# Attention on two 64-row halves of the TensorE array: scores and maximum's pass with one head of a pair on each half

## The chip, the cores and the metric

One NeuronCore of one Trainium2 chip runs the whole program. The metric is the device time of one execution in microseconds; the median of three runs is compared.

## The reference

Two layers of a diffusion backbone over 1024 latent tokens with a prefix of 256 context tokens, model width 1024, all in float32. Layer 0 mixes by recurrent heads and Fourier groups. Layer 1 is latent attention, and it alone is touched by the change. Cut to what matters:

```python
qc, kvc, kr, g = split(u @ w_in)              # 256, 128, 32, 1024 columns
q = rms_norm(qc) @ w_uq                       # 16 heads: 64 plain + 32 rotary dims
kv = rms_norm(kvc) @ w_ukv                    # 16 heads: 64 key dims + 64 value dims
q = concat(q[:64], rope(q[64:]))              # latent tokens only
k = concat(kv[:64], rope(kr))                 # rotary key: one for all heads
s = einsum('bqhd,bkhd->bhqk', q, k_all) * 96 ** -0.5   # 1024 queries x 1280 keys
o = softmax(s) @ v_all
y = (o * silu(g)) @ w_out
```

The layer ends with a gated residual and a layer norm; the output is the latent stream (1, 1024, 1024).

## The kernel before, in words

Everything is written with tile pools; a scheduler orders each engine's instructions and places the semaphores, starting from the order of the program text. Products that need float32 accuracy run as three float32r passes: both operands are split into a high and a low part (`split`, L85: a copy by one engine, L81 or L83, and a subtraction by another, L87), and high x high, high x low and low x high are summed (`mm3`, L89 to 92).

The stage of the gate columns (L977 to 994, line groups in1g) multiplies 8 blocks of weights by the latent activations, 384 matmuls of 512 columns in all. Between its steps a list `work` of closures prepares the first pair of heads (L973 to 975): weights and rotated queries of a quad of four heads (`prep_quad`), keys and queries of a pair (`prep_pair`), the maximum's pass (`max_pass`) and the quad's values (`prep_v`).

The attention (L1078 to 1126) runs over 8 pairs of heads, two halves of 512 queries, and 10 key tiles of 128 keys: 160 steps of `attend`. Keys lie on partitions of the scores. For each head of the pair a PSUM bank `s` takes three matmuls: high keys by high queries over 97 rows (64 plain dims, 32 rotary dims, and a row of ones in the keys that meets the negated maximum in the queries), high keys by low queries and low keys by high queries over 96 rows (L1021 to 1023). ScalarE's exponential writes a tile `p` (L1025; six buffers for each head), GpSimd adds it to the row sum `ra` (L1029), and P*V runs in plain float32 on two column halves of the array, one head on each (`tile_position=(0, 64 * a)`, L1034), in groups after the key tiles that `PVG` names (1, 3, 5, 7, 8) and after the last one. `finish` multiplies the row sums by ones on column halves (`rp`, L1059), inverts them on VectorE in four pieces (`ri`, L1066), multiplies by the gate (`sgt`, L1061 and L1070) and stores.

While a pair attends, the closures of the next pair are spread over the first 18 of its 20 steps, by the weights that stand beside them in the lists (L1087 to 1091). For odd `p` a new quad is prepared too. Each half of a pair thus has its own load: the first half holds the quad's rotations and the pair's keys and queries, the second mostly the maximum's pass and, with a quad, the values.

The pieces of a pair's preparation: `kn`, three chunks of keys (512, 512, 256 columns), each an `mm3` into one bank of `m_ps`, then for each head a 64-row split by ScalarE and VectorE; `qn`, two chunks of queries in the same way; `qr`, VectorE copies of the rotary queries (32 rows of 1024) into the rows 64 to 95 of `Qh` and `Ql` (L933, L934). The maximum's pass takes, for each head and each tile of 128 queries, the high x high scores against 512, 512 and 256 keys, one bank each (L955), reduces each bank to a maximum (L956) and the three to one (L957). `rows` transposes the maxima, negates them and sends them by a GpSimd DMA to the row 96 of `Qh` (L967).

PSUM has eight banks: four in `m_ps` (all preparations and the maximum's pass share them), three in `s_ps`, one in `o_ps`. The operands of a pair lie in `slots`: those of even pairs in the pool `prep`, those of odd pairs in the pool `at`. The pool `prep` is closed before the last pair (L1093). In the last pair nothing is prepared; instead `wo1_load` (L1101 to 1109) loads the output weights in eight pieces, multiplies them by the gate and splits them, all on VectorE, into tiles of a pool that is opened where `prep` lay, with two buffers `raw` for the pieces on their way. Loads and stores run on SyncE's queue (SP, `load`, L65).

Of the kernel before, what the change touches and what calls it, by code (L numbers as in the profile page):

```python
# [21 lines left out]
P = 128  # L22
# [32 lines left out]
MB = 4  # L55
SB = 3
# [3 lines left out]
def _body(ctx, tc, ap, out, dbg=None):  # L60
# [36 lines left out]
    # ---------------------------------------------------------------- constants  # L97
# [13 lines left out]
    # v = 8 softplus(-lambda): softplus(x) = max(x, 0) + log1p(exp(-|x|)),  # L111
    # log1p(e) = 2 atanh(e / (2 + e))
# [26 lines left out]
    # the channel DFT folded into the group weights  # L139
# [9 lines left out]
    # ---------------------------------------------------------------- adaLN  # L149
    # stationary: the silu of the two condition vectors, 32 columns (two used)  # L150
# [60 lines left out]
    # layer 0 by quarters of the channels, so that the projection can start on the first  # L211
# [4 lines left out]
    def ada_part(h):  # L216
# [12 lines left out]
        # chunk 2 s + i of shift (s = 0) and scale (s = 1): channel block 2 h + i  # L229
# [82 lines left out]
    # ---------------------------------------------------------------- RG-LRU heads  # L312
# [78 lines left out]
    # x projections run one head pair ahead of the gates that use them  # L391
# [3 lines left out]
    nop = lambda: None  # noqa: E731  # L395
# [435 lines left out]
    def slots(p, i0):  # L831
        for i in (i0, i0 + 1):
# [472 lines left out]
```

## Time and profile before

| | |
|---|---|
| median of 3 runs | 1498.38 us (1496.85 to 1505.64) |
| the profiled execution, first to last instruction | 1498.8 us |
| TensorE busy | 1434.9 us (96%) |
| VectorE, ScalarE, GpSimd busy | 1037.0, 571.7, 706.4 us |
| gate stage | 722 to 831 us |
| attention | 831 to 1400 us |

Busy times are unions of what the profiler recorded for an engine. A matmul's recorded end is modelled and lies behind the start of the next one, so the time that a matmul takes from a row of matmuls is read from start to start. PEld are weight loads. "Idle before" is the time that an engine stood before an instruction, with the instruction that ended the wait.

### The profile page before, as it was taken

Reading aid. Unit: us, or ns where it says so; the run is one execution under the profiler, and the core shown is the slowest. Engines: PE = TensorE matmul, PEld = TensorE weight load, DVE = VectorE, ACT = ScalarE, POOL = GpSimd, SP = SyncE. Lnnn points to the kernel's source line nnn. Section 1 sums busy time; section 2 is a strip of 40 time slices with the busy share of each in tenths; the row PEclk is TensorE's granted clock in tenths of the full one; section 3 lists DMA queues with packets and bytes.
Section 4 is the critical chain, followed back from the end, with each engine's and each line's share of the span. In section 5 each row is a group of like instructions: output and inputs, shape, how many; then the busy total and the mean of one; then the engine's idle time right before and its main releaser. Section 6 shows DMA issues by size and latency. Waiting matters only on the chain.

```text
span 1498.8 us, 18430 instructions
## 1 busy us (share of the span) xinstructions
PE 1434.9 (96%) x6880; PEld 1040.1 (69%) x6880; DVE 1037.0 (69%) x1636; ACT 571.7 (38%) x840; POOL 706.4 (47%) x460
## 2 busy tenths in 40 slices
PE   6998999999999999999999999999999999998898
PEld 3776777778888788879888655655566556554586
DVE  4669778765765243348675769787977787779498
ACT  2276565665113221124321544443444334443110
POOL 1135434343212154213411676677667756689652
PEclk9999999999999999999999999999999989999999
DMA  8613233332304653310231101010100000022542
GB/s 302 229 52 107 99 105 109 109 102 85 111 29 147 211 168 115 119 37 26 95 106 50 60 15 43 15 32 22 36 15 15 29 14 15 15 71 71 181 135 91
DMA packets 63641, 127.05 MB, mean 85 GB/s; under 512 B 5304, under 2 KB 31160, under 8 KB 61248
## 3 DMA queue, kind: packets, MB, share of 16 engines
q1 hardware_dynamic: 60592, 117.82, 24.1%
q0 software_dynamic: 2528, 7.67, 1.4%
q8 instruction: 54, 0.88, 0.3%
q10 hardware_dynamic: 432, 0.39, 0.1%
q14 instruction: 35, 0.29, 0.1%
HBM read 101.14 MB, written 24.66 MB: 84 GB/s over the span
## 4 chain that ended last, share of the span: by engine, by line
PE 72%; DVE 20%; DMA 3%; issue 2%; ACT 2%; POOL 1%; SPq 0%; DVEq 0%; ACTq 0%; POOLq 0%
PE z L272 13%; PE y L651 10%; PE po L1034 8%; PE yf L1167 6%; PE mx L955 5%; PE s L1021 4%; PE s L1023 4%; PE s L1022 4%; PE in1g L92 2%; PE in1g L90 2%; PE in1g L91 2%; DVE xc L322 2%; DVE th L367 1%; DVE gate L372 1%; DVE ri L1066 1%
## 5 line engine op out<-in xcount | busy, mean ns | idle before, releaser
L1029 POOL TENSOR_TENSOR ra<-ra,p 128x512 f32<-128x512 f32 x256 | 351.4, 1399 | 96.2 <-ACT p L1025 95.8
L1025 ACT ACTIVATE p<-s 128x512 f32<-128x512 f32 x320 | 190.1, 597 | 249.9 <-PE s L1023 222.2
L956 DVE TENSOR_REDUCE m<-mx 128x1 f32<-128x512 f32 (+1 forms) x384 | 207.8, 591 | 55.1 <-PE mx L955 53.8
L272 PE MATMUL z<-uh,w0h 128*128 128x512 f32 (+1 forms) x576 | 150.0, 367 | 4.3 <-ACT uh L81 4.3
L87 POOL TENSOR_TENSOR w0l<-w,w0h 128x1024 fp32r<-128x1024 f32 x24 | 63.9, 2664 | 184.5 <-DVE w0h L83 126.4
L272 PE MATMUL z<-uh,w0l 128*128 128x512 f32 (+1 forms) x576 | 147.7, 362 | 0.0
L272 PE MATMUL z<-ul,w0h 128*128 128x512 f32 (+1 forms) x576 | 147.7, 362 | 0.0
L1021 PE MATMUL s<-Qh,Kh 97*128 97x512 f32 x320 | 132.5, 414 | 6.3 <-ACT p L1025 6.3
L1022 PE MATMUL s<-Ql,Kh 96*128 96x512 f32 x320 | 128.1, 400 | 0.0
L1023 PE MATMUL s<-Qh,Kl 96*128 96x512 f32 x320 | 128.1, 400 | 0.0
L955 PE MATMUL mx<-Kh,Qh 96*128 96x512 f32 (+1 forms) x384 | 115.8, 376 | 7.9 <-DVE Ql L87 4.3
L272 PEld LDWEIGHTS z<-uh,w0h 128*128 128x128 f32 x576 | 98.4, 190 | 33.4 <-issue 10.7
L955 PEld LDWEIGHTS mx<-Kh,Qh 96*128 96x128 f32 x384 | 69.4, 190 | 66.2 <-issue 22.6
L272 PEld LDWEIGHTS z<-ul,w0h 128*128 128x128 f32 x576 | 96.7, 190 | 18.7 <-issue 1.0
L272 PEld LDWEIGHTS z<-uh,w0l 128*128 128x128 f32 x576 | 96.5, 190 | 18.4 <-issue 2.0
L350 ACT ACTIVATE gate<-gps,vec 128x512 f32<-128x512 f32 (+1 forms) x96 | 57.5, 616 | 103.6 <-PE gps L92 103.4
L1021 PEld LDWEIGHTS s<-Qh,Kh 97*128 97x128 f32 x320 | 60.9, 190 | 48.3 <-issue 24.9
L1034 PE MATMUL po<-p,v_even 128*64 128x512 f32 x320 | 85.9, 620 | 0.0
L1034 PE MATMUL po<-p,v_odd 128*64 128x512 f32 x320 | 82.7, 615 | 0.0
L1029 POOL TENSOR_TENSOR ra<-p,p 128x512 f32<-128x512 f32 x32 | 48.4, 1533 | 70.6 <-ACT p L1025 70.6
L386 POOL TENSOR_TENSOR gate<-gate,gate 128x1280 f32<-128x1280 f32 x8 | 23.9, 2992 | 112.2 <-DVE gate L383 97.1
L1023 PEld LDWEIGHTS s<-Qh,Kl 96*128 96x128 f32 x320 | 61.7, 193 | 15.7 <-issue 3.2
(357 smaller groups left out, 2983.3 us busy)
## 6 DMA issues: line engine op xcount, KB each, us to landing
w<-in_w SPq DMA_DIRECT2D x24, 512.0 KB, 4.4
adaw<-in_ada SPq DMA_DIRECT2D x32, 256.0 KB, 4.9
adawm<-in_ada SPq DMA_DIRECT2D x8, 1024.0 KB, 5.7
adawg<-in_ada_g SPq DMA_DIRECT2D x8, 1024.0 KB, 4.9
y_dr<-sg SPq DMA_DIRECT2D x10, 640.0 KB, 5.5
woraw<-in_wo SPq DMA_DIRECT2D x12, 512.0 KB, 3.6
xt<-in_x_cm SPq DMA_DIRECT2D x8, 640.0 KB, 6.4
yra<-y_dr SPq DMA_DIRECT2D x10, 512.0 KB, 4.8
```

Of the source, the lines that this page charges most:

```text
L87: el.tensor_tensor(out=lo, in0=src, in1=f(hi), op=ALU.subtract)
L272: TE.matmul(z[:, a : a + n], wi[:, kt, :], ui[kt][:, a : a + n], start=(kt == 0 and ui is uh and wi is wh), stop=(kt == KT - 1 and wi is wl))
L651: TE.matmul(ps[:, 512 * hf : 512 * hf + 512], a[k], b[k][:, 512 * hf : 512 * hf + 512], start=(k == 0 and a is yh and b is woh), stop=(k = ...
L955: TE.matmul(ps[:, :n], Qh[s][0:96, P * t : P * t + P], Kh[s][0:96, a0 : a0 + n], start=True, stop=True)
L956: V.tensor_reduce(out=m3[:, i : i + 1], in_=ps[:, :n], axis=AX.X, op=ALU.max)
L1021: TE.matmul(ps, Kh[s][0:97, ks], Qh[s][0:97, c], start=True, stop=False)
L1022: TE.matmul(ps, Kh[s][0:96, ks], Ql[s][:, c], start=False, stop=False)
L1023: TE.matmul(ps, Kl[s][:, ks], Qh[s][0:96, c], start=False, stop=True)
L1025: S.activation(out=e, in_=ps, func=AF.Exp, scale=SCALE)
L1029: G.tensor_tensor(out=ra, in0=st["e"][0][a] if kt == 1 else ra, in1=e, op=ALU.add)
L1034: TE.matmul(st["o"][64 * a : 64 * a + 64, :], quad[q][6][:, k, 128 * i + 64 * a : 128 * i + 64 * a + 64], st["e"][k][a], start=(k == 0), s ...
L1167: TE.matmul(ps[i], a[:, k, :], b[k][:, pieces[i]], start=(k == 0 and a is oh and b is w1o), stop=(k == 7 and a is ol))
```

## The change

The two heads of a pair lie on two halves of the array's rows: partitions 0 to 63 hold the first head, 64 to 127 the second, in `Qh`, `Ql`, `Kh`, `Kl`, which now carry the 64 plain dims alone. The rotary dims and the maximum move into tiles of their own. `KR1` holds for each half the 32 high rows of the rotary key and its 32 low rows, `R1` the high rotary query twice, so that one matmul over 64 rows gives high x high and high x low. `KR2` holds the high rotary key and rows of ones, `R2` the low rotary query and the negated maximum, over 33 rows. A step of `attend` becomes five parts, each two matmuls (one per head) on the two row halves, into the two banks of one tile `s`; one exponential, one tile `p` and one row sum serve both heads. In the last pair the sum of the second head goes to VectorE. The maximum's pass runs plain and rotary part (`Qh` x `Kh`, `R1` x `KR1`) for both heads into two banks `x`, and one reduction serves both heads. Its unit is now one chunk of keys: 24 units a pair. Splits of keys and queries take both heads at once. Rotary queries are brought by six DMAs of 32 rows on SyncE's queue, rotary keys by three. PSUM: `m_ps` has one bank `m` for the preparations and two for `x`, one buffer of each; `s_ps` two buffers of two banks. The output weights' high parts are copied by ScalarE. Lines that change comments alone are left out.

```diff
-MB = 4
-SB = 3
...
-    m_ps, m_psc = pool("m_ps", MB, space=PSUM)
-    s_ps, s_psc = pool("s_ps", SB, space=PSUM)
+    m_ps, m_psc = pool("m_ps", 1, space=PSUM)
+    s_ps, s_psc = pool("s_ps", 2, space=PSUM)
...
+    def slots(p, i):
+        Qh[i] = p.tile([P, NL], F32R, name=f"Qh{i}")
+        Ql[i] = p.tile([P, NL], F32R, name=f"Ql{i}")
+        Kh[i] = p.tile([P, T], F32R, name=f"Kh{i}")
+        Kl[i] = p.tile([P, T], F32R, name=f"Kl{i}")
+        R1[i] = p.tile([P, NL], F32R, name=f"R1{i}")
+        R2[i] = p.tile([P, NL], F32R, name=f"R2{i}")
+    def rotary_keys():
+        for a in range(2):
+            V.memset(f(KR2)[64 * a + 32 : 64 * a + 64, :], 1.0)
+        S.copy(out=KR1[64:96, :], in_=kr_t[64:96, :])
+        V.tensor_tensor(out=KR1[96:128, :], in0=kr_t[64:96, :], in1=f(KR1)[64:96, :], op=ALU.subtract)
+        load(f(KR1)[0:64, :], f(KR1)[64:128, :])
+        for a in range(2):
+            load(f(KR2)[64 * a : 64 * a + 32, :], f(KR1)[64:96, :])
     pr_p, pr_c = pool("prep", side="left")
+    KR1 = pr_p.tile([P, T], F32R, name="KR1")
+    KR2 = pr_p.tile([P, T], F32R, name="KR2")
...
     def prep_pair(p):
-                for a in range(2):
-                    split(Qh[sl[a]][0:64, c], Ql[sl[a]][0:64, c], pq[64 * a : 64 * a + 64, :], S, V)
+                split(Qh[b][:, c], Ql[b][:, c], pq, S, V)
...
         def qr():
             for a in range(2):
                 g = slice(64 * i + 32 * a, 64 * i + 32 * a + 32)
-                V.tensor_copy(out=Qh[sl[a]][64:96, :], in_=f(roth)[g, :])
-                V.tensor_copy(out=Ql[sl[a]][64:96, :], in_=f(rotl)[g, :])
+                for r in range(2):
+                    load(f(R1[b])[64 * a + 32 * r : 64 * a + 32 * r + 32, :], f(roth)[g, :])
+                load(f(R2[b])[64 * a : 64 * a + 32, :], f(rotl)[g, :])
...
-                for a in range(2):
-                    split(Kh[sl[a]][0:64, a0 : a0 + n], Kl[sl[a]][0:64, a0 : a0 + n], pk[64 * a : 64 * a + 64, :n], S, V)
+                split(Kh[b][:, a0 : a0 + n], Kl[b][:, a0 : a0 + n], pk[:, :n], S, V)
-        return [(kn(a0, n), 1.3) for a0, n in CH3] + [(qn(0), 1.5), (qr, 2.2), (qn(1), 1.5)]
+        return [(qr, 0.0)] + [(kn(a0, n), 0.9) for a0, n in CH3] + [(qn(0), 1.5), (qn(1), 1.5)]
     def max_pass(p):
-        def unit(a, t):
+        def unit(t, i):
             def run():
+                if i == 0:
+                    m3s[t] = pr_p.tile([P, 2, 3], F32, tag="m3", bufs=3, name=f"m3{p}{t}")
+                a0, n = CH3[i]
+                ps = m_ps.tile([P, 2, 512], F32, tag="x", name=f"mx{p}{t}{i}")
+                for q, k, st in ((Qh[b], Kh[b], True), (R1[b], KR1, False)):
+                    for a in range(2):
+                        r = slice(64 * a, 64 * a + 64)
+                        TE.matmul(ps[:, a, :n], q[r, P * t : P * t + P], k[r, a0 : a0 + n], start=st, stop=not st)
+                V.tensor_reduce(out=m3s[t][:, :, i], in_=ps[:, :, :n], axis=AX.X, op=ALU.max)
+                if i == 2:
+                    V.tensor_reduce(out=nm[:, :, t], in_=m3s[t], axis=AX.X, op=ALU.max)
...
-                G.dma_start(out=Qh[s][96:97, :], in_=row[8 * a : 8 * a + 8, :])
+                G.dma_start(out=R2[b][64 * a + 32 : 64 * a + 33, :], in_=row[8 * a : 8 * a + 8, :])
-        return [(unit(a, t), 2.0) for t in range(8) for a in range(2)] + [(rows, 0.5)]
+        return [(unit(t, i), 1.0 if i == 2 else 1.6) for t in range(8) for i in range(3)] + [(rows, 0.5)]
+    slots(pr_p, 0)
-    work = (work[:1] + wait + [(lambda: trq(TOKE[-1]), 0.0), (lambda: slots(pr_p, 0), 0.0)] + wait[:W2]
+    work = (work[:1] + wait + [(lambda: trq(TOKE[-1]), 0.0), (rotary_keys, 0.0)] + wait[:W2]
...
+        sp = s_ps.tile([P, 2, 512], F32, tag="s", name=f"in1g{m}")
         for q in range(2):
-            ps = s_ps.tile([P, 512], F32, tag="s", name=f"in1g{m}{q}")
+            ps = sp[:, q, :]
...
     def attend(p, hf, kt, st):
-        for a in range(2):
-            s = 2 * (p % 2) + a
-            ps = s_ps.tile([P, 512], F32, tag="s", name=f"s{p}{hf}{kt}{a}")
-            TE.matmul(ps, Kh[s][0:97, ks], Qh[s][0:97, c], start=True, stop=False)
-            TE.matmul(ps, Kh[s][0:96, ks], Ql[s][:, c], start=False, stop=False)
-            TE.matmul(ps, Kl[s][:, ks], Qh[s][0:96, c], start=False, stop=True)
...
+        ps = s_ps.tile([P, 2, 512], F32, tag="s", name=f"s{p}{hf}{kt}")
+        parts = ((Kh[b], Qh[b], 64), (Kh[b], Ql[b], 64), (Kl[b], Qh[b], 64), (KR1, R1[b], 64), (KR2, R2[b], 33))
+        for j, (k, w, n) in enumerate(parts):
+            for a in range(2):
+                r = slice(64 * a, 64 * a + n)
+                TE.matmul(ps[:, a, :], k[r, ks], w[r, c], start=(j == 0), stop=(j == len(parts) - 1))
+        es = at.tile([P, 2, 512], F32, tag="p", bufs=PB, name=f"p{p}{hf}{kt}")
+        S.activation(out=es, in_=ps, func=AF.Exp, scale=SCALE)
+        if kt:
+            ra = st["ra"]
+            for eng, h in ((G, slice(0, 2)),) if p < 7 else ((G, slice(0, 1)), (V, slice(1, 2))):
+                eng.tensor_tensor(out=ra[:, h], in0=(st["e"][0] if kt == 1 else ra)[:, h], in1=es[:, h], op=ALU.add)
...
-                    split(w1o[k], w1p[k], r, V, V)
+                    split(w1o[k], w1p[k], r, S, V)
```

## Rows read from the trace of the kernel before

**Rows 1.** The page, part 1: busy us, share of the span, instructions.
```profile
PE 1434.9 (96%) x6880; PEld 1040.1 (69%) x6880; DVE 1037.0 (69%) x1636; ACT 571.7 (38%) x840; POOL 706.4 (47%) x460
```

**Rows 2.** Windows: gate stage, then attention by half; us, busy us (instructions), clock, DMA, GB/s.
```profile
722.10:831.10 109.00, 109.00 (x504) 90.19 (x503) 66.27 (x140) 29.38 (x52) 28.00 (x23) 1.00 0.27 86
...
896.40:938.10 41.70, 38.85 (x153) 22.96 (x153) 34.90 (x54) 17.35 (x32) 24.69 (x19) 0.96 0.12 38
...
1119.10:1153.00 33.90, 33.90 (x144) 20.12 (x145) 25.74 (x45) 17.70 (x31) 26.76 (x21) 1.00 0.05 16
1153.00:1184.70 31.70, 31.70 (x136) 18.22 (x137) 23.07 (x47) 12.53 (x21) 24.48 (x21) 1.00 0.06 18
1184.70:1229.40 44.70, 41.86 (x153) 24.17 (x154) 34.99 (x54) 17.43 (x32) 24.83 (x19) 0.89 0.07 24
...
1331.80:1357.70 25.90, 25.90 (x105) 13.44 (x106) 24.37 (x18) 12.42 (x21) 23.60 (x13) 1.00 0.36 117
1357.70:1399.80 42.10, 30.42 (x105) 14.39 (x106) 32.82 (x20) 13.27 (x23) 41.24 (x25) 0.84 0.28 81
```

**Rows 3.** Timeline of TensorE, last pair: start us, us, engine line op names count.
```profile
1378.45 1.94 PE L1034 MATMUL po<-p,v_odd 128*64 128x512 f32 x8
1380.32 0.50 PE L1021 MATMUL s<-Qh,Kh 97*128 97x512 f32 x1
1380.66 0.40 PE L1022 MATMUL s<-Ql,Kh 96*128 96x512 f32 x1
1380.89 0.40 PE L1023 MATMUL s<-Qh,Kl 96*128 96x512 f32 x1
...
1386.46 0.39 PE L1023 MATMUL s<-Qh,Kl 96*128 96x512 f32 x1
1386.78 1.08 PE L1034 MATMUL po<-p,v_odd 128*64 128x512 f32 x4
1387.79 0.50 PE L1021 MATMUL s<-Qh,Kh 97*128 97x512 f32 x1
```

**Rows 4.** Tile po: count, duration ns min/median/max, first and last start.
```profile
L1034 PEld LDWEIGHTS po<-p,v_odd x320: 132/136/232, 979.2 to 1398.4; 128*64 128x64 f32 x160
L1034 PE MATMUL po<-p,v_odd x320: 592/592/1112, 979.2 to 1399.1; 128*64 128x512 f32 x160
```

**Rows 5.** Timeline of TensorE's weight loads, 1003 to 1005 us.
```profile
1003.59 0.20 PEld L1034 LDWEIGHTS po<-p,v_odd 128*64 128x64 f32 x4 [0.36 <-issue]
```

**Rows 6.** Tile mx: reductions, and what its engine waited for (us, times).
```profile
L956 DVE TENSOR_REDUCE m<-mx x384: 404/677/693, 768.9 to 1324.3; 128x1 f32<-128x512 f32 x128, 128x1 f32<-128x256 f32 x64
...
  DVE m L956: 19.0, 33
```

**Rows 7.** Groups by line, 831.1 to 1401.6 us: busy us, mean ns, idle before.
```profile
L87 DVE TENSOR_TENSOR Kl<-pk,Kh 64x512 fp32r<-64x512 f32 (+1 forms) x42 | 24.2, 596 | 4.9 <-ACT Kh L81 4.3
...
L933 DVE CAST Qh<-roth 32x1024 fp32r<-32x1024 f32 x14 | 18.8, 1342 | 0.3
...
L934 DVE CAST Ql<-rotl 32x1024 fp32r<-32x1024 f32 x14 | 15.0, 1071 | 18.5 <-PE s L1022 18.4
```

**Rows 8.** Tile sgt: its loads and stores, issue to landing.
```profile
DMA to landing us min/median/max: 2.0/2.0/2.9
```

**Rows 9.** Timeline of GpSimd, 1327 to 1401 us.
```profile
1327.50 5.01 POOL L1029 TENSOR_TENSOR ra<-ra,p 128x512 f32<-128x512 f32 x4
...
1337.94 32.33 POOL L1029 TENSOR_TENSOR ra<-ra,p 128x512 f32<-128x512 f32 x16
```

**Rows 10.** Timeline of VectorE, start of the last pair.
```profile
1332.43 0.69 DVE L1061 TENSOR_TENSOR sgt<-sgt,osb 128x512 f32<-128x512 f32 x1 [6.26 <-ACT osb L1047]
1333.92 1.23 DVE L1107 TENSOR_TENSOR w1oraw<-w1oraw,g1bc 128x1024 f32<-128x1024 f32 x1 [0.80 <-DMA w1oraw<-in_wo]
...
1336.75 2.30 DVE L1107 TENSOR_TENSOR w1oraw<-w1oraw,g1bc 128x1024 f32<-128x1024 f32 x1
```

**Rows 11.** Timeline of TensorE, end of the last pair, with idle before.
```profile
1395.01 0.80 PE L1021 MATMUL s<-Qh,Kh 97*128 97x512 f32 x1 [6.26 <-ACT p L1025]
```

More of the change, by code (lines that the diff above doesn't have):

```diff
@@ L822, in _body @@
     e_psc()
-    m_ps, m_psc = pool("m_ps", MB, space=PSUM)
-    s_ps, s_psc = pool("s_ps", SB, space=PSUM)
-    Qh, Ql, Kh, Kl = {}, {}, {}, {}
-    def slots(p, i0):
-        for i in (i0, i0 + 1):
-            Qh[i] = p.tile([97, NL], F32R, name=f"Qh{i}")
-            Ql[i] = p.tile([96, NL], F32R, name=f"Ql{i}")
-            Kh[i] = p.tile([97, T], F32R, name=f"Kh{i}")
-            Kl[i] = p.tile([96, T], F32R, name=f"Kl{i}")
-            if i == 0:
-                for t in range(NT):
-                    G.tensor_copy(out=Kh[0][96:97, P * t : P * t + P], in_=one)
-                S.copy(out=Kh[0][64:96, :], in_=kr_t[64:96, :])
-                V.tensor_tensor(out=Kl[0][64:96, :], in0=kr_t[64:96, :], in1=f(Kh[0])[64:96, :], op=ALU.subtract)
-            else:
-                e = G if i == 1 else V
-                e.tensor_copy(out=Kh[i][64:97, :], in_=f(Kh[0])[64:97, :])
-                e.tensor_copy(out=Kl[i][64:96, :], in_=f(Kl[0])[64:96, :])
+    m_ps, m_psc = pool("m_ps", 1, space=PSUM)
+    s_ps, s_psc = pool("s_ps", 2, space=PSUM)
+    Qh, Ql, Kh, Kl, R1, R2 = {}, {}, {}, {}, {}, {}
+    def slots(p, i):
[13 more added lines that the diff above has]
+            load(f(KR2)[64 * a : 64 * a + 32, :], f(KR1)[64:96, :])
     pr_p, pr_c = pool("prep", side="left")
-    one = pr_p.tile([1, P], F32, name="one")
-    V.memset(one, 1.0)
+    KR1 = pr_p.tile([P, T], F32R, name="KR1")
+    KR2 = pr_p.tile([P, T], F32R, name="KR2")
     vt = {0: pr_p.tile([P, NT, 256], F32, name="v_even")}
@@ L917, in prep_pair @@
         wh, wl, kh, kl, roth, rotl, v = quad[q]
[L918 removed]
+        b = p % 2
         def qn(hf):
@@ L1000, in _body @@
     o_ps, o_psc = pool("o_ps", 1, space=PSUM)
-    slots(at, 2)
+    slots(at, 1)
     ones = at.tile([P, 64], F32, name="ones")
@@ L1014, in attend @@
             st["o"] = o_ps.tile([P, 512], F32, tag="o", name=f"po{p}{hf}")
-            st["ra"] = [at.tile([P, 512], F32, tag=f"ra{a}", bufs=2, name=f"ra{p}{hf}{a}") for a in range(2)]
+            st["ra"] = at.tile([P, 2, 512], F32, tag="ra", bufs=2, name=f"ra{p}{hf}")
             st["e"] = []
-        es = []
-        for a in range(2):
-            s = 2 * (p % 2) + a
-            ps = s_ps.tile([P, 512], F32, tag="s", name=f"s{p}{hf}{kt}{a}")
-            TE.matmul(ps, Kh[s][0:97, ks], Qh[s][0:97, c], start=True, stop=False)
-            TE.matmul(ps, Kh[s][0:96, ks], Ql[s][:, c], start=False, stop=False)
-            TE.matmul(ps, Kl[s][:, ks], Qh[s][0:96, c], start=False, stop=True)
-            e = at.tile([P, 512], F32, tag=f"p{a}", bufs=PB, name=f"p{p}{hf}{kt}{a}")
-            S.activation(out=e, in_=ps, func=AF.Exp, scale=SCALE)
-            es.append(e)
-            if kt:
-                ra = st["ra"][a]
-                G.tensor_tensor(out=ra, in0=st["e"][0][a] if kt == 1 else ra, in1=e, op=ALU.add)
+        b = p % 2
+        ps = s_ps.tile([P, 2, 512], F32, tag="s", name=f"s{p}{hf}{kt}")
[10 more added lines that the diff above has]
+                eng.tensor_tensor(out=ra[:, h], in0=(st["e"][0] if kt == 1 else ra)[:, h], in1=es[:, h], op=ALU.add)
         st["e"].append(es)
@@ L1034, in pv @@
                 TE.matmul(st["o"][64 * a : 64 * a + 64, :], quad[q][6][:, k, 128 * i + 64 * a : 128 * i + 64 * a + 64],
-                          st["e"][k][a], start=(k == 0), stop=(k == NT - 1), tile_position=(0, 64 * a))
+                          st["e"][k][:, a, :], start=(k == 0), stop=(k == NT - 1), tile_position=(0, 64 * a))
         if pend and kt == DK:
@@ L1058, in rows @@
             for a in range(2):
-                TE.matmul(st["rp"][64 * a : 64 * a + 64, :], ones, st["ra"][a], start=True, stop=True, tile_position=(0, 64 * a))
+                TE.matmul(st["rp"][64 * a : 64 * a + 64, :], ones, st["ra"][:, a, :], start=True, stop=True, tile_position=(0, 64 * a))
             st["ri"] = at.tile([P, 512], F32, tag="ri", name=f"ri{p}{hf}")
```

10 lines of the change are left out of this document (2 added, 8 removed).

## The prediction

> **What bounds the kernel now.** I read the page's engine shares first, then the attention's halves in a table of windows, then single instructions. TensorE is busy 96% of the span [rows 1]. The stage of the gate columns (722 to 831 us) is TensorE without a gap, 109.00 us busy of 109.00 [rows 2]. In the attention the half of a pair is the unit. Halves that prepare a pair without a new quad take 33.9 and 31.7 us, all of it TensorE, with VectorE at 25.7 and 23.1 us [rows 2]. Three halves prepare a quad as well (the first and the last of them stand in the rows): 41.7, 40.2 and 44.7 us, VectorE with 35 us of work and TensorE idle for 2.8 us in each [rows 2]. The last pair is different again: 25.9, then 42.1 us with GpSimd busy 41.24 us [rows 2].
>
> So most halves are the sum of their matmuls. A 512-column score matmul takes a slot of 0.23 us (start to start), although each is recorded at 0.40 us [rows 3]. The switches into and out of the column-tiled P*V groups cost extra: the last score starts 0.32 us before the group, not 0.23 (+0.09); four P*V matmuls take 1.01 us to the next start while four more add only 0.86 (+0.15); the first score after it takes 0.34 (+0.11). Together 0.35 us a visit [rows 3].
>
> **Do two tiles of the array run side by side?** No instruction of this kernel uses row halves, but P*V uses column halves. Eight of its records take 1.87 us to the next start, 0.23 each [rows 3]. One is recorded at 592 ns [rows 4]; less the tail of 0.16 us that scores show (0.40 against 0.23) it holds its half for 0.43 us, so two overlap fully. Weight loads do too: four of 136 ns fit into 0.20 us [rows 4, 5]. I take the same of row halves and 0.005 us more a slot: 0.236 us for one step of both heads. Bounds: 0.231 (free) and 0.462 (one after the other).
>
> **The change, part by part** (sums against this execution's span, 1498.8 us; the runs' median is 1498.38, so nothing is added).
>
> *Scores.* Six slots per key tile become five: 6 x 0.231 = 1.386, 5 x 0.236 = 1.18, so 0.206 us. In pairs 0 to 6 there are 140 key tiles: **-28.8 us**. Weight loads double (ten per 1.18 us), but two halves load at once as column halves do [rows 5].
>
> *Maximum's pass.* Before, one matmul per head and chunk; now two steps that both heads share: the same TensorE time. VectorE's 48 reductions a pair become 24 over both heads. 512 columns take 677 ns and 256 take 404 [rows 6], so 1.07 ns a column: 1024 should take 1.22 us. A pair's reductions go from 32 x 0.677 + 16 x 0.404 = 28.1 us to 16 x 1.22 + 8 x 0.677 = 24.9.
>
> *VectorE.* Per pair also five splits of 64 rows fewer (5 x 0.6 = 3.0 us) and no rotary copies (2 x 1.34 + 2 x 1.07 = 4.8 us), and the 18.4 us that VectorE stood before those copies until old scores had ended go too [rows 7]. With the reductions that is 11 us a pair. The halves that prepare a quad hold about 101 slots of 0.231, 8 of 0.117, 44 of 0.217 and 7 visits of 0.35, so 36.2 us; they lose 5.5, 4.0 and 8.5 us to VectorE, 18 in all. I give back **-15** (bounds 0 and -18).
>
> *Rotary rows by DMA.* Six copies a pair on SP's queue. A load of this stage lands 2.0 us after issue [rows 8]; the first group of the maximum's pass needs it, but three key and two query products come between. For an even pair SP waits until VectorE has split the rotated queries, and the next rope tables and gate tiles queue behind; none of these is wanted sooner than some us. I count nothing; if the cover fails it is 2 us in four pairs at most.
>
> *More visits.* Key, query, rotation, value and transpose products stay on the full array and now interrupt row-tiled work. In pairs 1 to 7 that is 7 x 6 + 3 x 7 = 63 groups. Where a group follows P*V it costs half a visit, else a whole one: I take 0.28 us, **+17.6** (bounds 0.17 and 0.35 each: 11 and 22). In the gate stage, which has no slack, 24 groups of the maximum's pass sit between full-array products: 24 x 0.35 = **+8.4** (bounds 4 and 10).
>
> *One buffer for the maximum's pass.* Before, four banks turn over; now one pair of banks, and one bank for all preparations. A 512-column group holds its banks for 0.236 to its last start, 0.393 until that ends and 1.22 for the reduction, 1.85 us; a 256 one 1.07. A pair's 24 groups chain to 38 us; the four preparations ahead of the first group, one buffer each in turn (product, ScalarE copy, VectorE subtraction, about 2.1 us), add 8. VectorE's other 13 us fit between at best. That makes 46 to 59 us beside 63 us of TensorE work in a plain pair (65.6 - 4.1 + 6 x 0.3), so it fits, but not everywhere: with four buffers 33 groups already waited for the reduction, 0.58 us each [rows 6]. There are 24 units on 18 steps, so one in three is second in its step. 56 groups at half that wait: **+16** (bounds 0 and 168 x 0.58 = 97).
>
> The Trainium skill's "TensorEngine Tiling (Array Packing)", section Performance Considerations, says that tiling speeds up TensorE but not the emptying of PSUM, which may become the limit. It speaks against this edit: by it the 24 reductions set a pair's pace, the slower rival below. The plain halves before don't show it, VectorE has room there [rows 2].
>
> *Last pair.* GpSimd's 36 sums take 1.25 us alone (four in 5.01) and 2.02 here (16 in 32.33) [rows 9]; VectorE's products of two tensors take 1.23 alone and 2.30 here [rows 10]. Each waits for the other's instruction. TensorE then stands 6.26 us for exponentials that wait for buffers [rows 11], and its granted clock falls (0.84 on average over that half, so a part of it at 1.2 GHz [rows 2]). Now GpSimd keeps 18 sums (22.5 us), VectorE gets 18 (0.69 each, as its product of this size at 1332 us [rows 10]: 12.4) beside 16 x 1.23 and four short products (22.5), and ScalarE takes the 8 casts. The shared time falls from 45 + 22.5 = 67.5 us (68.0 measured) to 57, and the casts no longer delay either; TensorE's own work is 47 us. I take the middle, 52: **-16** (bounds -11 and -21). One thing goes the other way: the rotary keys lie in the pool that is closed before this pair, and the pair still reads them. If the output weights that take their place must wait, two staging buffers are held and 19.6 us of VectorE work move behind the attention, beside the first product tile's 48 slots, 11 us: then the upper end is about -5.
>
> Sum: -28.8 - 15 + 17.6 + 8.4 + 16 - 16 = -17.8, so **1481 us**.
>
> **Rivals.**
> 1. *The reductions pace the pairs (slower).* TensorE issues in order; if two groups in three wait 0.58 us, 112 x 0.58 = 65 us instead of 16: **1530 us**. It decides from 35 us of such waits on (60 groups). For it: one buffer, other VectorE work of 0.7 to 1.7 us between the reductions. Against: VectorE falls to about 38 of 63 us in a plain pair.
> 2. *No waits.* Preparations land behind P*V groups (visits 8 us cheaper), the buffers never bind (16), and the last pair is TensorE's 47 us (5 more): **1452 us**. For it: the plain halves before lose next to nothing.
> 3. *The quad halves don't relax.* The single bank for rotations and keys (7 products of some 3 us in turn, 21 us, in a third of a half) takes the place of VectorE's load: the -15 goes, **1496 us**, no measurable change.
> 4. *The halves don't overlap as hoped.* If not at all: 1.13 us more in each of 160 key tiles (181) and 9 us per maximum's pass of eight (72): 1734 us. If only in part, say 0.30 us a step because weight loads are exposed (a first score after a visit, with its load exposed, takes 0.34): 0.064 x 800 = 51 and 20 in the maximum's passes: 1552 us. Against both: the column halves overlap fully [rows 3 to 5].
>
> The Trainium skill's "TensorE: Matmul & The Clock Gate", Part 3 (Measured speedup vs the span model), gives 3.07 for four row tiles and 2.38 for three column tiles, 0.78 of the ideal. By that rule a step would take 0.231 / 0.78 = 0.296 us (an estimate), about the partial case; this trace's sustained column halves don't bear it out.
>
> **Chances.** Forecast 0.43 (its own range 1466 to 1494; a little over half of it is below the bound for faster), rival 1: 0.19, rival 2: 0.20, rival 3: 0.10, rival 4: 0.08 (0.05 in part). A measurement of this kernel can tell about 1% (15 us) from no change. Faster by over 1%: 0.25 of the forecast and rival 2, 0.45. Within 1%: the rest of the forecast, rival 3 and the lower edge of rival 1, 0.30. Slower: 0.25. The range that leaves out 2 in 10 goes from rival 2 to rival 1: 1450 to 1532.
>
> **What would show it.** Right: score matmuls in pairs a few ns apart, a pair every 0.23 to 0.24 us; plain pairs near 64 us, the quad halves near 37; VectorE waiting more and TensorE's waits before the maximum's pass near 0.1 us a group; the gate stage some 8 us longer; the last pair near 52 us. Wrong: a step of 0.3 us or more; gaps before most groups of the maximum's pass, ended by its reduction; output weights split after the last score.

## The result and the profile after

The changed kernel takes 1662.92 us (median of four runs, 1659.55 to 1665.39) against 1497.62 of the kernel before in the same session: ratio 1.1081, 95% interval 1.1041 to 1.1122. It is slower, and 131 us above the upper end of the predicted range. The profiled executions span 1657.5 and 1498.8 us, so 158.7 us are to be found.

To find them I cut each span at the same events: the first product of the gate columns, the last copy of P\*V sums (ScalarE's osb) of pair 6 and of pair 7, and the end. Every kernel of this study is listed with these three stretches (us):

| kernel | gate stage and pairs 0 to 6 | last pair | after it | span |
|---|---|---|---|---|
| before | 609.6 | 68.0 | 99.0 | 1498.8 |
| changed | 748.0 | 48.2 | 137.9 | 1657.5 |
| e1 keys open | 750.4 | 68.8 | 104.2 | 1655.1 |
| e2 short reductions | 699.0 | 48.3 | 136.2 | 1608.5 |
| e3 three banks | 686.7 | 48.2 | 137.7 | 1597.3 |
| e4 two edits, last pair | 611.2 | 61.9 | 103.2 | 1499.9 |
| e5 shared tiles, full array | 803.9 | 81.6 | 106.3 | 1720.8 |
| e6 row halves, own tiles | 650.0 | 53.9 | 136.5 | 1563.2 |
| e7 cast held back | 609.6 | 54.2 | 114.7 | 1499.9 |
| e8 held and lagged | 603.5 | 60.0 | 97.6 | 1485.3 |
| e9 e6 with the end mended | 648.6 | 66.1 | 104.1 | 1545.3 |
| e10 e6, even chunks | 646.0 | 53.9 | 137.1 | 1559.2 |

The experiments e1, e2, e3, e5, e6 and e10 were run once. In before, e4, e7 and e8 nothing is edited up to pair 6, and that stretch still differs by 7.7 us between their executions (603.5 to 611.2), so differences of that size say nothing.

The change loses 138.4 us up to pair 6, wins 19.8 in the last pair, and loses 38.9 behind it. First the page's engine shares of the changed kernel, to be held beside [rows 1]: VectorE has 78 us less to do, and still everything is later.

```profile
PE 1506.9 (91%) x7904; PEld 1018.7 (61%) x7904; DVE 958.9 (58%) x1315; ACT 535.1 (32%) x648; POOL 630.7 (38%) x304
```

The windows of the changed kernel answer to [rows 2]: the gate stage with pairs 0 to 6, one half that prepares a quad, two plain halves, the two halves of the last pair, and the gap behind it (us; then busy us of TensorE, weight loads, VectorE, ScalarE, GpSimd; granted clock; DMA share; GB/s).

```profile
723.40:1471.40 748.00, 675.15 (x3515) 360.04 (x3517) 386.97 (x489) 205.19 (x245) 336.20 (x157) 0.97 0.13 39
928.50:980.00 51.50, 44.59 (x214) 21.21 (x214) 31.38 (x37) 13.56 (x16) 22.39 (x10) 0.93 0.16 46
1210.90:1255.80 44.90, 38.91 (x207) 19.38 (x209) 23.00 (x26) 13.38 (x17) 24.72 (x12) 0.96 0.08 22
1255.80:1293.80 38.00, 32.89 (x203) 16.42 (x203) 21.13 (x26) 10.81 (x11) 22.25 (x12) 1.00 0.04 15
1471.40:1495.60 24.20, 24.20 (x146) 11.50 (x148) 14.37 (x15) 10.81 (x12) 14.80 (x10) 1.00 0.06 22
1495.60:1519.60 24.00, 23.81 (x143) 11.29 (x143) 13.86 (x15) 10.83 (x11) 13.85 (x10) 1.00 0.17 55
1519.60:1557.90 38.30, 1.08 (x4) 0.20 (x4) 23.67 (x23) 9.99 (x10) 0.69 (x1) 0.58 0.41 139
```

The kernel before in the gate stage with pairs 0 to 6:

```profile
722.20:1331.80 609.60, 599.88 (x2571) 380.81 (x2570) 453.24 (x830) 249.21 (x432) 378.03 (x295) 0.99 0.11 36
```

Of the 138.4 us lost there, TensorE's idle time makes up 63.1 (9.7 before, 72.9 now). In the other 75.3 it is recorded as busy, so waits alone are less than half of the loss.

Plain halves that were TensorE without a gap (33.9 and 31.7 us) now take 44.9 and 38.0, with idle time of 5 to 6 us in each. The timeline of TensorE in another plain half shows where it sits (start us, us recorded, engine, line, operation, names, count; in brackets idle time and what ended it):

```profile
1448.52 0.39 PE L962 MATMUL mx<-Kh,Qh 64*128 64x256 f32 x2
1448.74 0.28 PE L962 MATMUL mx<-KR,R 64*128 64x256 f32 x2
1448.86 0.39 PE L1033 MATMUL s<-Qh,Kh 64*128 64x512 f32 x2
1449.09 0.39 PE L1033 MATMUL s<-Ql,Kh 64*128 64x512 f32 x2
1449.32 0.40 PE L1033 MATMUL s<-Qh,Kl 64*128 64x512 f32 x2
1449.56 0.39 PE L1033 MATMUL s<-R,KR 64*128 64x512 f32 x1
1451.57 0.50 PE L962 MATMUL mx<-Kh,Qh 64*128 64x512 f32 x2 [1.62 <-DVE m L963]
1451.90 0.39 PE L962 MATMUL mx<-KR,R 64*128 64x512 f32 x2
```

VectorE over the same stretch, in the same columns:

```profile
1447.68 1.75 DVE L1076 RECIPROCAL ri<-rp 128x128 f32<-128x128 f32 x2
1449.47 1.44 DVE L1080 TENSOR_TENSOR sgt<-ri,sgt 128x512 f32<-128x512 f32 x1
1450.83 0.68 DVE L963 TENSOR_REDUCE m<-mx 128x2 f32<-128x512 f32 x1
```

Read the two together. The group of 1448.52 has left the array by about 1449, but its reduction starts at 1450.83, because two reciprocals and a product stand ahead of it on VectorE. Until it ends, the one buffer is held. The next group stands in TensorE's order in the middle of a key tile's scores (seven of its ten matmuls have started by 1449.56), so the other scores wait with it. The tile mx of the changed kernel shows how often (idle time of the engines before its instructions, what ended it, us and times), beside [rows 6]:

```profile
L963 DVE TENSOR_REDUCE m<-mx x192: 629/1224/1228, 765.9 to 1464.4; 128x2 f32<-128x1024 f32 x128, 128x2 f32<-128x512 f32 x64
its engine sat idle before it (us, times) until:
  PE mx L962: 168.5, 154
  DVE m L963: 144.7, 188
```

TensorE's own part of the second row:

```profile
PE mx L962 <- DVE m L963: 44.8, 80, 3.4
```

In 154 of 192 groups VectorE stands and waits for the matmuls, 168.5 us in all. The other way round a reduction is waited for 188 times, 144.7 us: 44.8 us in 80 waits of TensorE's matmuls, the rest in its weight loads. The two take turns. Behind the last pair the timeline of ScalarE shows the output weights' casts, each waiting for VectorE's product of weights that have just been loaded:

```profile
1523.56 2.17 ACT L79 CAST w1oh<-w1oraw 128x1024 fp32r<-128x1024 f32 x2 [3.36 <-DVE w1oraw L1117]
1531.72 1.04 ACT L79 CAST w1oh<-w1oraw 128x1024 fp32r<-128x1024 f32 x1 [5.98 <-DVE w1oraw L1117]
...
1556.82 1.04 ACT L79 CAST oh<-orw 128x1024 fp32r<-128x1024 f32 x1 [4.19 <-DMA orw<-o_dr]
```

The last row is the cast of the first output tile. Its load takes one of the two buffers that the weights' pieces pass through and was issued at 1552.71 us, when the pieces were split, so it comes late with them.

The timeline of TensorE shows what that costs, 36.49 us until the first output product:

```profile
1557.91 1.22 PE L1177 MATMUL yf<-w1oh,oh 128*128 128x512 f32 x2 [36.49 <-ACT oh L79]
```

### The profile page after: what moved, and what is told of

Its sections match the earlier page's. It is cut to its first block, busy times and chain, and to the rows that moved or that the text cites. A ratio compares the mean times of both kernels' runs of the same rounds, so it can differ in the third digit from the quotient of the medians.

```text
span 1657.5 us, 19613 instructions
## 1 busy us (share of the span) xinstructions
PE 1506.9 (91%) x7904; PEld 1018.7 (61%) x7904; DVE 958.9 (58%) x1315; ACT 535.1 (32%) x648; POOL 630.7 (38%) x304
## 4 chain that ended last, share of the span: by engine, by line
PE 67%; DVE 24%; DMA 3%; ACT 2%; issue 2%; POOL 1%; SPq 0%; DVEq 0%; ACTq 0%; POOLq 0%
PE z L270 12%; PE po L1044 9%; PE y L649 9%; PE s L1033 7%; DVE m L963 7%; PE mx L962 6%; PE yf L1177 6%; DVE ri L1076 2%; PE in1g L88 2%; PE in1g L89 2%; PE in1g L90 2%; DVE xc L320 2%; DVE gate L370 1%; DVE th L365 1%; PE rp L1069 1%
## 5 line engine op out<-in xcount | busy, mean ns | idle before, releaser
L1039 POOL TENSOR_TENSOR ra<-ra,p 128x1024 f32<-128x1024 f32 (+1 forms) x128 | 291.3, 2276 | 236.4 <-ACT p L1035 234.3
L963 DVE TENSOR_REDUCE m<-mx 128x2 f32<-128x1024 f32 (+1 forms) x192 | 200.3, 1043 | 168.6 <-PE mx L962 168.5
L1035 ACT ACTIVATE p<-s 128x1024 f32<-128x1024 f32 x160 | 164.0, 1025 | 374.8 <-PE s L1033 373.5
L1033 PE MATMUL s<-R,KR 33*128 33x512 f32 (+1 forms) x640 | 134.3, 405 | 0.0
L962 PE MATMUL mx<-Kh,Qh 64*128 64x512 f32 (+1 forms) x384 | 92.9, 453 | 45.2 <-DVE m L963 44.8
L1033 PE MATMUL s<-Qh,Kh 64*128 64x512 f32 x320 | 87.9, 447 | 0.0
L1033 PEld LDWEIGHTS s<-R,KR 33*128 33x128 f32 (+1 forms) x640 | 76.9, 190 | 15.7 <-issue 2.2
L1033 PE MATMUL s<-Ql,Kh 64*128 64x512 f32 x320 | 82.8, 402 | 0.0
L1033 PE MATMUL s<-Qh,Kl 64*128 64x512 f32 x320 | 79.8, 403 | 0.0
L962 PE MATMUL mx<-KR,R 64*128 64x512 f32 (+1 forms) x384 | 77.3, 360 | 0.0
```

Source lines behind the costliest of these rows:

```text
L962: TE.matmul(ps[:, a, :n], q[r, P * t : P * t + P], k[r, a0 : a0 + n], start=st, stop=not st)
L963: V.tensor_reduce(out=m3s[t][:, :, i], in_=ps[:, :, :n], axis=AX.X, op=ALU.max)
L1033: TE.matmul(ps[:, a, :], k[r, ks], w[r, c], start=(j == 0), stop=(j == len(parts) - 1))
L1035: S.activation(out=es, in_=ps, func=AF.Exp, scale=SCALE)
L1039: eng.tensor_tensor(out=ra[:, h], in0=(st["e"][0] if kt == 1 else ra)[:, h], in1=es[:, h], op=ALU.add)
```

## The experiments

**e1: the rotary keys in a pool that stays open.**

```diff
+    kr_p, kr_c = pool("keys", side="left")
+    KR1 = kr_p.tile([P, T], F32R, name="KR1")
+    KR2 = kr_p.tile([P, T], F32R, name="KR2")
     pr_p, pr_c = pool("prep", side="left")
-    KR1 = pr_p.tile([P, T], F32R, name="KR1")
-    KR2 = pr_p.tile([P, T], F32R, name="KR2")
```

> The changed kernel with the two rotary-key tiles KR1 and KR2 in a pool of their own that stays open to the end; nothing else differs. Theory A (the output weights take the place of KR1 and KR2, which the last scores still read, so the weights' casts and splits come only after the last score): the idle time of 36.5 us before the first output product goes, the stretch from the last score to the end falls from 137 to about 100 us, and the last pair grows by 0 to 4 us because weights are now split beside it; span 1657 to 1621-1630. Rival (the weights are late because their loads stand behind others on SyncE's queue, or because ScalarE and VectorE are full in the last pair): at most 10 us less, span 1647 or more, with the casts of w1oh still after the last exponential.

Measured: 1657.21 us in one run, span 1655.1. The weights do move into the last pair and what follows it falls from 137.9 to 104.2 us, as theory A had it. But the pair grows from 48.2 to 68.8 us, not by 0 to 4, so 13.1 of the 33.7 us stay (the gate stage also began 8.3 us later in this execution, which hides most of them in the span). ScalarE's timeline in e1's last pair tells why:

```profile
1499.87 1.03 ACT L1036 ACTIVATE p<-s 128x1024 f32<-128x1024 f32 x1 [0.65 <-PE s L1034]
1505.72 1.04 ACT L79 CAST w1oh<-w1oraw 128x1024 fp32r<-128x1024 f32 x1 [4.82 <-DVE w1oraw L1118]
1506.67 1.02 ACT L1036 ACTIVATE p<-s 128x1024 f32<-128x1024 f32 x1
```

Its row in the table of waits (us in total, times, longest):

```profile
ACT w1oh L79 <- DVE w1oraw L1118: 17.3, 6, 5.2
```

A cast that waits for VectorE stands ahead of exponentials: 17.3 us in six waits. The last pair's gain was that the weights were not there.

**e2: short reductions.** Most of the maximum is left out.

```diff
-                V.tensor_reduce(out=m3s[t][:, :, i], in_=ps[:, :, :n], axis=AX.X, op=ALU.max)
+                V.tensor_reduce(out=m3s[t][:, :, i], in_=ps[:, :, :64], axis=AX.X, op=ALU.max)
...
-        S.activation(out=es, in_=ps, func=AF.Exp, scale=SCALE)
+        S.activation(out=es, in_=ps, func=AF.Exp, scale=SCALE / 4)
```

> The changed kernel, where the maximum's reduction reads only the first 64 columns of each head's chunk instead of 512 or 256, so most of the maximum is left out; the exponential's scale is a quarter, so that nothing overflows. The matmuls, their weights, the visits of the pass and its buffer stay as they are; only the time for which its one PSUM buffer is held shrinks, by about 0.8 us of a mean 1.04 in 192 groups. Theory B (the one buffer makes matmuls and reduction take turns): the pairs 0 to 6 fall from 84 (plain) and 99 (quad) us to about 70 and 84, some 90 us together, and the gate stage loses 5 to 10; span 1657 to 1550-1580. Rival C (the time is in the visits themselves: changes between full, row and column modes, and products of weights by values cut in pieces): under 20 us less, span 1637 or more.

Measured: 1610.63 us; gate stage and pairs 0 to 6 take 699.0 us, 49.0 less. That is far over rival C's 20 and well short of theory B's 77 to 107. The tile mx of e2:

```profile
L963 DVE TENSOR_REDUCE m<-mx x192: 228/292/295, 769.4 to 1417.2; 128x2 f32<-128x128 f32 x192
...
  PE mx L962: 235.4, 163
```

With reductions of 0.29 us the buffer still makes the two engines take turns (VectorE waits 163 times), as the reduction's place in VectorE's order is unchanged. So shorter reductions give back half of the 98 us that the shared tiles cost (e6 below). That is more than the time for which the buffer is held: VectorE's work in this stretch also falls, from 387.0 to 253.1 us, and all that stands behind a reduction comes sooner.

**e3: three single banks.** The pass, the preparations and the row sums share a ring of three banks, each head reduced on its own.

```diff
-    m_ps, m_psc = pool("m_ps", 1, space=PSUM)
+    m_ps, m_psc = pool("m_ps", 3, space=PSUM)
...
-                ps = m_ps.tile([P, 2, 512], F32, tag="x", name=f"mx{p}{t}{i}")
+                ps = [m_ps.tile([P, 512], F32, tag="m", name=f"mx{p}{t}{i}{a}") for a in range(2)]
...
+                for a in range(2):
+                    V.tensor_reduce(out=m3s[t][:, a, i : i + 1], in_=ps[a][:, :n], axis=AX.X, op=ALU.max)
```

> The changed kernel, where the maximum's pass writes each head's scores to a one-bank PSUM tile of its own, in a ring of three banks that the preparations and row sums share (the same banks that were one for these and two for the pass); each head has its own reduction, 384 of 0.68 or 0.40 us in place of 192 of 1.22 or 0.63. Theory B (turns through one buffer): the next group's first head finds a free bank at once and the second waits only for one reduction, so a part of the turns goes: 30 to 70 us less, span 1590-1630, unless VectorE's added instructions (192 by about 0.15, 29 us in all, over seven pairs in which it is half idle) take it back. Rival C (visits): no gain, span 1650 or more.

Measured: 1599.65 us, 686.7 up to pair 6: 61.3 less, with the same number of banks and more reductions. TensorE's waits for the pass fall from 44.8 us (80 times) to 16.9, while the ring brings a new wait (TensorE's waits in e3, us in total, times, longest):

```profile
PE pk L88 <- DVE ri L1077: 17.0, 3, 5.7
PE mx L962 <- DVE m L964: 16.9, 34, 4.4
```

**e4: the two edits of the last pair alone, in the kernel before.**

```diff
-                G.tensor_tensor(out=ra, in0=st["e"][0][a] if kt == 1 else ra, in1=e, op=ALU.add)
+                (V if p == 7 and a else G).tensor_tensor(out=ra, in0=st["e"][0][a] if kt == 1 else ra, in1=e, op=ALU.add)
...
-                    split(w1o[k], w1p[k], r, V, V)
+                    split(w1o[k], w1p[k], r, S, V)
```

> The kernel before with two edits of the change alone: in the last pair the second head's row sums go to VectorE instead of GpSimd, and the output weights' first cast goes to ScalarE instead of VectorE. Scores, layouts and PSUM stay as before. Theory D (the last pair is paced by GpSimd's additions, 36 of 1.2 us, and the change's 20 us there come from these two edits and not from the row halves): the last pair falls from 68 to 48-53 us, and the time by 15 to 20 us, to 1478-1483. Rival (the last pair gains by the five steps in place of six slots and by exponentials of two heads together): the pair stays above 60 us, the time above 1490.

Measured: 1497.57 us, ratio 0.9991 (0.9967 to 1.0016): nothing. The pair takes 61.9 us instead of 68.0, and what follows 103.2 instead of 99.0. Theory D falls. The rival's numbers hold, but its reason doesn't: in e1 the five steps and shared exponentials are there and the pair takes 68.8 us. Common to both is the weights' work.

**e5 and e6: the change in two parts.** e5 puts the kernel before on the change's PSUM tiles, e6 puts the change's row halves on the tiles of before (its row sums stay over both heads). First e5, on the kernel before:

```diff
-MB = 4
-SB = 3
+MB = 1
+SB = 2
...
+                ps = m_ps.tile([P, 2, 512], F32, tag="x", name=f"mx{p}{t}{i}")
+                    TE.matmul(ps[:, a, :n], Qh[s][0:96, P * t : P * t + P], Kh[s][0:96, a0 : a0 + n], start=True, stop=True)
...
+        sp = s_ps.tile([P, 2, 512], F32, tag="s", name=f"s{p}{hf}{kt}")
+        S.activation(out=es, in_=sp, func=AF.Exp, scale=SCALE)
```

Then e6, on the changed kernel, beside e3's edit of the pass:

```diff
+    m_ps, m_psc = pool("m_ps", 4, space=PSUM)
+    s_ps, s_psc = pool("s_ps", 3, space=PSUM)
...
+        ps = [s_ps.tile([P, 512], F32, tag="s", name=f"s{p}{hf}{kt}{a}") for a in range(2)]
+            S.activation(out=es[:, a, :], in_=ps[a], func=AF.Exp, scale=SCALE)
```

> The kernel before with the change's PSUM tiles alone: both heads of a pair in one two-bank tile (two for scores, one for the maximum's pass, one bank for preparations and row sums), exponentials, row sums and reductions over both heads at once. Operands and matmuls stay on the full array, with six slots a key tile. Theory B (the turns through the pass's one buffer are the main loss): pairs 0 to 6 take 590 to 640 us in place of 501, the time is 1590-1650. Rival C (the loss comes with the row halves: changes of mode, halves that run alone): pairs 0 to 6 stay under 530 us, the time under 1535.

> The change's row halves alone: its operands and matmuls, but each head with one-bank PSUM tiles as before (four that the maximum's pass, preparations and row sums share, three for scores), exponentials and reductions by head. Theory B: without the one buffer pairs 0 to 6 come back to 490-530 us (501 before, 634 with the change), the last pair stays near 48 and the tail near 138, the time is 1505-1555. Rival C: pairs 0 to 6 stay at 560 us or more, as with three shared banks, the time at 1590 or more.

Measured: e5 1722.62 us, e6 1565.26. Theory B's side of both; e5 is worse than it said (pairs 0 to 6 alone take 694.5 us), and e6 just above its range (531.7). Gate stage and pairs 0 to 6 make a square (us):

| | four banks in a ring, scores in three | one shared buffer and one bank, scores in two pairs |
|---|---|---|
| full array | 609.6 (before) | 803.9 (e5) |
| row halves | 650.0 (e6) | 748.0 (changed) |

Sharing the tiles costs 98 us with row halves and 194 without. The halves cost 40 us where there are banks enough and give back 56 where there aren't. VectorE has less work with them (387 us against e5's 447), which may be why; no run shows it. The window of that stretch in e5, where the granted clock is 0.92:

```profile
729.00:1532.90 803.90, 727.95 (x2565) 405.74 (x2565) 447.41 (x561) 225.54 (x285) 345.95 (x167) 0.92 0.09 28
```

TensorE's largest wait in it, summed:

```profile
PE mx L959 <- DVE m L960: 33.5, 28, 2.2
```

The same window and waits of e6:

```profile
722.80:1372.80 650.00, 616.12 (x3517) 361.58 (x3517) 391.29 (x692) 214.89 (x393) 336.88 (x157) 0.98 0.15 45
```

```profile
PE pq L88 <- DVE ri L1077: 16.0, 3, 5.3
PE mx L962 <- DVE m L964: 9.2, 17, 1.7
```

With four banks the pass waits 9.2 us in 17 places, but the queries of three quads still wait 5.3 us each for a bank that the row sums hold until VectorE's reciprocals are done.

Where the time lies can be summed from the traces. Each of TensorE's matmuls is given the time to the start of the next one, less idle time (us, gate stage and pairs 0 to 6):

| | before | e6 | changed |
|---|---|---|---|
| TensorE idle | 9.7 | 33.9 | 72.9 |
| scores | 211.6 | 195.0 | 222.1 |
| maximum's pass | 83.5 | 102.4 | 101.6 |
| P\*V and row sums | 151.6 | 152.9 | 181.3 |
| gate columns and preparations | 153.1 | 165.9 | 170.1 |

Of the 98 us between e6 and the changed kernel, idle time is 39.0. Scores (27.1) and P\*V with row sums (28.4) take most of the rest, though their matmuls are the same in number.

**e7 and e8: the last pair of before again.** Both have VectorE's row sums from e4 and hold back a cast that the trace shows in the wrong place: before, the cast of the first output tile is queued ahead of the last exponentials and waits 9.3 us for its load, and the 6.26 us of [rows 11] end with the exponential behind it. ScalarE's timeline of before:

```profile
1393.42 1.04 ACT L81 CAST oh<-orw 128x1024 fp32r<-128x1024 f32 x1 [9.34 <-DMA orw<-o_dr]
1394.37 1.56 ACT L1025 ACTIVATE p<-s 128x512 f32<-128x512 f32 x3
```

e8 has e4's cast on ScalarE too, two key tiles later.

```diff
+        with tc.issue_after(exp_last[0]) if t == 0 else ExitStack():
+            split(oh, ol, orw, S, V)
```

And in e8 alone:

```diff
-                    split(w1o[k], w1p[k], r, V, V)
+            def wo1_split(k):
+                return lambda: split(w1o[k], w1p[k], w1r[k], S, V)
...
+                steps[min(4 + 2 * k, 2 * NT - 1)].append(wo1_split(k))
```

> The kernel before with two edits in the last pair: the second head's row sums on VectorE, and the cast of the first output tile queued on ScalarE behind the last exponential. The output weights' cast stays on VectorE. Theory D2 (the last pair of before waits twice: for GpSimd's sums, 5.4 us, and for a cast that stands ahead of exponentials and waits for its load, 9.3 us on ScalarE and 6.3 on TensorE; and a cast of weights on ScalarE holds exponentials in the same way, which took the gain of the run with the first two edits): the pair falls from 68 to 52-56, the time by 10 to 15, to 1483-1488. Rival (the output weights' work on VectorE paces the pair as soon as GpSimd doesn't): the pair at 60 or more, the time within 5 us of before.

> As the run with VectorE's row sums and the cast behind the last exponential, and also the output weights' cast on ScalarE, but issued two key tiles after the product that it needs, so that it does not stand waiting ahead of exponentials. Theory D2: ScalarE waits under 2 us for VectorE's products (7.8 us when cast at once), the pair takes 50 to 54 us, the time is 1480-1485, some 3 us under the run with VectorE's casts. Rival: the order comes out the same as before, the waits stay and the time is within 5 us of before.

Measured: e7 1501.54 us, ratio 1.0013 (0.9988 to 1.0037); e8 1490.75 us, ratio 0.9955 (0.9936 to 0.9973). e7's pair falls to 54.2 us as D2 said and nothing is won: what follows grows from 99.0 to 114.7: TensorE waits 8.3 us for the last row sums, which on VectorE stand behind the weights' work, and then 4.3 us for the first output tile's cast. In e8 the pair and the rest take 157.6 us together against 167.0 before, with TensorE busy 57.03 of the pair's 60.0 us (the other 4.1 us between the spans lie before pair 7, where nothing is edited). e8's windows of the pair and of what follows:

```profile
1327.70:1387.70 60.00, 57.03 (x212) 27.43 (x212) 55.29 (x46) 32.32 (x52) 29.41 (x19) 1.00 0.32 99
1387.70:1485.30 97.60, 90.12 (x409) 73.31 (x408) 82.48 (x96) 11.48 (x18) 42.14 (x16) 0.98 0.42 143
```

ScalarE's largest wait in that pair, summed:

```profile
ACT w1oh L81 <- DVE w1oraw L1109: 13.2, 7, 3.1
```

D2's mechanism is not borne out (ScalarE still waits 13.2 us for products); yet e8 is faster than both kernels, by 0.45% of the one before. Which of holding and lagging does it together with e4's edits was not separated.

**e9: e6 with e1's pool and e8's end.** The edits are those shown above.

> The row halves with one-bank tiles (as in the run that kept the PSUM of before), and at the end of the attention three edits: KR1 and KR2 in a pool that stays open, the output weights' casts issued two key tiles after their products, the first output tile's cast queued behind the last exponential. Theory A with D2 (at the end two things cost: weights that wait for the rotary keys, and casts that stand waiting ahead of exponentials): the last pair goes from 54 to 56-62 us, the tail from 136 to 97-103, the time from 1565 to 1528-1540. Above before all the same, since gate stage and pairs 0 to 6 take 650 us in place of 610. Rival: weights and row halves get in each other's way in the last pair (as with the keys alone, where it took 69 us): 1545 or more.

Measured: 1548.41 us, ratio 1.0322 (1.0281 to 1.0363): the time is on the rival's side. The pair takes 66.1 us, above theory A's 62 and below the rival's 69, and the rest 104.1; 20 us of the end are mended. Up to pair 6 nothing changes (648.6 us), and the row halves stay slower than before.

**e10: even chunks in e6.**

```diff
-                a0, n = CH3[i]
+                a0, n = ((0, 432), (432, 432), (864, 416))[i]
```

> The row halves with one-bank tiles, where the maximum's pass cuts the 1280 keys into 432, 432 and 416 columns instead of 512, 512 and 256; columns and instructions stay the same in number. Theory E (a step of 256 columns on row halves can't be shorter than the load of its weights: 0.22 us from the first step to the next, where its columns need 0.117): the 64 groups of 256 columns lose about 0.1 us each, and steps of 416 and 432 columns run at 0.19 to 0.20; gate stage and pairs 0 to 6 take 5 to 10 us less than 650. Rival: the step after fills the gap already, or the waits decide: under 2 us of difference.

Measured: 1561.29 us; 646.0 us up to pair 6, 4.0 less. That lies between theory E's 5 to 10 and the rival's 2, and within the 7.7 us by which an unedited stretch differs between executions, so the time decides nothing. But the timeline of e6 refutes theory E's premise:

```profile
1352.78 0.39 PE L962 MATMUL mx<-Kh,Qh 64*128 64x256 f32 x2
1353.00 0.28 PE L962 MATMUL mx<-KR,R 64*128 64x256 f32 x2
1353.12 0.97 PE L962 MATMUL mx<-Kh,Qh 64*128 64x512 f32 x2
```

The second step of 256 columns takes 0.12 us to the next start; the first, behind P\*V, takes 0.22. A first score step behind such column-tiled matmuls is longer by as much: 0.33 us to the next start in e6 (1368.98 to 1369.31) instead of 0.23.

## Why the prediction was wrong, point by point

- **Do the halves overlap? Right.** The pairs above start 0.23 us apart (1448.86, 1449.09, 1449.32), both heads under one start; I took 0.236. Rival 4 falls. The Trainium skill's "TensorE: Matmul & The Clock Gate", Part 3, would have it at an estimated 0.296 us; this trace disagrees.
- **VectorE's reductions: right in size.** 1.224 us for 1024 columns (1.22 predicted), 0.68 for 512 in the row of 1450.83 (0.68).
- **"One buffer for the maximum's pass: +16": wrong, the main error.** All the shared tiles together cost +98 us (748.0 against e6's 650.0). Cutting the banks of the pass and the preparations anew gives back 61.3 of them (e3), nearly four times the forecast; the other 37, with a fourth bank and one-bank score tiles, were not taken apart. The chain of 38 us a pair assumed that a reduction starts when its matmuls end. It starts when VectorE comes to it, behind reciprocals, gate products and splits, and the waiting group holds back the scores queued behind it. The row that the term was scaled from was misread as well: of its 33 waits (19.0 us) 32 are weight loads' (18.0 us) and one is a matmul's (1.0 us), and in the changed kernel the same row stands at 188 waits and 144.7 us. Rival 1 named the mechanism, at 65 us for this wait. It too counts waits alone, but in 59 of the 98 us TensorE is recorded as busy. A lower clock (last section) and matmuls that lose their partner on the other half (the single one at 1449.56 above) are seen there; how the 59 us divide between them stays open. The Trainium skill's "TensorEngine Tiling (Array Packing)", Performance Considerations, warns that the emptying of PSUM may become the limit. The direction agrees; yet VectorE is busy only 387 of the 748 us, and half of the loss stays when the reductions are short (e2), so their rate is not all of it.
- **"Scores -28.8, quad halves -15, more visits +17.6, gate stage +8.4": together -17.8 predicted, +40.4 measured** (e6 against before, each with four and three banks). The gate stage came out as forecast: 118.3 us in e6 against 108.9, +9.4. The scores win 16.6 us, not 28.8. The maximum's pass and the gate columns with the preparations take 18.9 and 12.8 us more, 31.7 against the 26.0 forecast for visits and gate stage. And idle time grows by 24.2 us where 15 were to be given back: this is the step that failed. The quad halves don't relax. In the changed kernel the row sums wait 14.7 us in three places for the one bank that the rotations hold, rival 3's mechanism at its price of 15; in e6 the queries wait 16.0 us for a bank that the row sums hold.
- **"Last pair: -16": right by the row (48.2 us, 19.8 less), wrong in its reason.** The two edits give nothing alone (e4). The pair was short because the weights' work had left it. And the 6.26 us of [rows 11], which I put down to buffers that GpSimd holds, fall in a wait of ScalarE for a load, with a cast queued ahead of the exponential. With that cast held back and half of the sums on VectorE (e7) TensorE no longer waits for an exponential in that pair. As GpSimd's sums ran until 1394.25 us beside that wait, and no run holds back the cast alone, the share of the buffers stays open.
- **"If the output weights that take their place must wait ... the upper end is about -5": mis-sized.** It happened, and pair and rest together take 186.1 us against 167.0: +19.1, not -5. I had hidden that VectorE work beside the first product tile, but TensorE started on the output only when weights and tile were cast: 36.49 us idle.

The 98.0 and the 40.4 are the two parts of the 138.4 us of the first stretch. With the 19.1 they make 157.5 of the spans' 158.7 us; by the other 1.2 us the gate stage starts later.

## What to carry to other kernels

A shared buffer's hold ends when the draining engine's queue reaches the drain, so price it by what stands ahead there, and price the wait by what stands behind the waiting matmul in TensorE's order; merging two small tiles into one big one trades instructions for exactly this slack. A stage that becomes short may have lost its work to the next one: judge the two together. Before a tile is put into a pool, look at who takes its place and when its last reader runs.

## What the hardware showed that was not expected

A wait costs again after it has ended. In the changed kernel the row sums wait 4.90 us, and the timeline of TensorE then runs:

```profile
941.65 1.97 PE L1069 MATMUL rp<-ra,ones 128*64 128x512 f32 x4 [4.90 <-DVE rc L893]
943.56 0.79 PE L1033 MATMUL s<-Qh,Kh 64*128 64x512 f32 x2
944.15 0.63 PE L1033 MATMUL s<-Ql,Kh 64*128 64x512 f32 x2
944.58 0.63 PE L1033 MATMUL s<-Qh,Kl 64*128 64x512 f32 x2
```

The row sums are recorded at 1.97 us (1.08 in the last pair) and a score step takes 0.43 instead of 0.23. The windows of these stretches have the granted clock in the third column from the end:

```profile
941.60:943.50 1.90, 1.85 (x4) 0.32 (x4) 1.06 (x2) 0.00 (x0) 0.00 (x0) 0.50 0.64 163
943.50:945.80 2.30, 2.30 (x12) 1.49 (x10) 2.14 (x3) 0.00 (x0) 0.00 (x0) 0.55 0.62 208
945.80:949.00 3.20, 3.20 (x16) 1.26 (x14) 3.17 (x4) 1.02 (x1) 1.84 (x1) 1.00 0.73 164
```

After the idle time it is at the lower level, 1.2 GHz, and then at the full one again. Over the 748.0 us the granted clock is 0.97 on average, in e5's 803.9 us 0.92, in before's 609.6 us 0.99. At two levels of full and half speed, 0.97 means 6% of the time, 45 us, at the lower one, which loses at most some 22 us; by the same working e5 loses at most 64 and before 6 (estimates from these means). The sum had no term for this.
